# RWKV-7 scan in chunks of 64 tokens in place of 32, inside a two-layer hybrid diffusion block

## The chip, the cores and the metric

One NeuronCore of a Trainium2 chip runs the whole program: TensorE (PE) does the matrix products, VectorE (DVE), ScalarE (ACT) and GpSimd (POOL) the rest, SyncE (SP) and ACT issue the DMAs. The metric is the time of the whole program on the device in microseconds, smaller is better: 1599.16 us before, the median of three runs (1598.88 to 1600.44).

## The reference, cut to what matters

Two layers, each a mixer with four branches and a feed-forward part, are applied to 128 context tokens and 256 latent tokens. Branch A of the mixer is an RWKV-7 scan in both directions, with 4 heads of 64 channels. For each direction and head it is

```python
def step(S, inp):
    r_t, w_t, k_t, v_t, kk_t, a_t = inp
    s_a = jnp.einsum('dbhvk,dbhk->dbhv', S, -kk_t)
    S = (S * w_t[..., None, :] + s_a[..., :, None] * (kk_t * a_t)[..., None, :]
         + v_t[..., :, None] * k_t[..., None, :])
    return S, jnp.einsum('dbhvk,dbhk->dbhv', S, r_t)
S_fin, ys = lax.scan(step, S0, xs)
```

The context scan starts from zero, the latent scan from a cached state. The branches B, C and D are attentions; all four are multiplied by branch weights, gated, summed and projected.

## The kernel before, in words

All 384 tokens are worked on together. The large products (`gemm`, L686 to L688; the branch products, L882 to L884) split each fp32 weight tile into a high part (`whi`, made on ACT, L419) and a low part (`wlo_`, made on DVE or POOL, L421) and use three 128x128 products with 384 moving columns for each; below they are called **wide** products. `split_to` keeps four half tiles ready ahead of PE (HB = 4).

The mixer is a main generator (`main`: input projection, gates, branch products, in the order D, C, B, A) and two side generators, `side_rwkv` and `side_attention`. `run` advances the sides between steps of the main one; each `yield n` of a side says how many main steps it lets pass, stretched by PACE_RW or PACE_AT. The framework then orders the instructions of each engine; every engine runs its own list in order. Branch A is the last that `main` needs (`ready`, L870).

`side_rwkv` runs `rwkv_pair` for two pairs of heads in each layer, four times in all. In a pair, head 0 has its channels in partitions 0 to 63 and head 1 in 64 to 127 (`par` in the code). The tokens are cut into 12 chunks of 32 for each direction. The stages of a pair:

- **preparation** (L1230 to L1321): decays, their running sums, and the scaled keys. `KR` holds for each chunk 32 columns of kk and 32 of r (L1298, L1299), `BK` 32 columns of the b vectors and 32 of k (L1316, L1317).
- **chunk products** (L1327 to L1335): `AM` = BK^T KR for each chunk and head, 64x64, masked by L1334; then BK is transposed into `BKT` (L1344 to L1357), and `v` is loaded beside it into `UV`.
- **inverse** (L1336 to L1392): the 32x32 triangular block of each of 48 systems goes through DRAM into a layout with one system per partition, is inverted on DVE by 31 steps of a multiply (L1382) and a subtract (L1384), and goes through DRAM into `qt`.
- **scan** (L1399 to L1460): 8 steps. In steps 0 to 3 four scans are in flight (2 directions, latent and context), in steps 4 to 7 two. A step of n scans has five groups of 2n small fp32 products: KR^T S (L1409) and AM^T v (L1414) into one bank; copy to `rs` (L1417); qt^T rs (L1425); copy to UV with a minus (L1426 on ACT for head 0, L1427 on DVE for head 1); BKT^T UV (L1435) for the new state and AM^T u (L1442) for the outputs; then the state's sum and scaling (L1445, L1446) and the copy of the outputs (L1448).
- **end** (L1463 to L1511): both directions are added, normalised and gated; after branch C has been used, L1198 transposes the result for the branch product.

In the profile an fp32 product counts as two matmul instructions, so a group of 8 products is shown as x16.

Of the kernel before, what the change touches and what calls it, by code (L numbers as in the profile page):

```python
# [21 lines left out]
NP = 128  # L22
# [9 lines left out]
GATE_ORDER = (BR_D, BR_C, BR_B, BR_A)  # L32
LAG = 2
# [138 lines left out]
C_MASK, C_SCAN = 960, 1024  # L172
C_FLIP = 1408
NCONST = 1536


def constants():
# [29 lines left out]
    s = (p % 32)[:, None]  # L207
    j = np.arange(32)[None]
    c[:, C_MASK:C_MASK + 32] = s < j
    c[:, C_MASK + 32:C_MASK + 64] = s <= j  # L210
    c[:, C_SCAN:C_SCAN + NT] = (np.arange(NT) % 32 != 0)[None]
# [116 lines left out]
def build(tc, I, O):  # L328
# [451 lines left out]
    def mixer(l, x, xspill, hs, M, merged_of):  # L780
# [10 lines left out]
        vB = M.tile([128, 3, 384], F32, name="vB")  # L791
# [414 lines left out]
        def chunk(g, d, i):  # L1206
            if d == 0:
                return (4 + i) if g == 0 else i
            return i if g == 0 else 8 + i
# [7 lines left out]
        def slot0(i):  # L1217
            return i * 4 if i < 4 else 16 + (i - 4) * 2

        def rwkv_pair(pr):  # L1220
# [3 lines left out]
            def t6(name):  # L1224
                return M.tile([128, 2, 12, 64], F32, name=name, tag="t6", bufs=4)

            def flat(t, d):
                return t[:, d, :]
# [36 lines left out]
            gs = M.tile([128, 24], F32, name="gs", tag="gs", bufs=2)  # L1265
            for d in range(2):
                for g in range(2):
                    n = 8 if g == 0 else 4
                    if d == 0:
                        base, step = (128 + 31, 32) if g == 0 else (31, 32)  # L1270
                    else:
                        base, step = (352, -32) if g == 0 else (96, -32)
                    idx = g * 2 + d

                    def src(a, b):
                        lo = base + step * a
                        hi = base + step * (b - 1)
                        if step > 0:
                            return lw[:, d, 1 + lo:2 + hi:32]
                        return lw[:, d, 1 + hi:2 + lo:32][:, ::-1]  # L1280

                    V.tensor_copy(gs[:, idx:16:4], src(0, 4))
                    if g == 0:
                        V.tensor_copy(gs[:, 16 + idx:24:2], src(4, 8))
# [4 lines left out]
            def view(t, d, part):  # L1289
                v = t[:, d, :, part * 32:part * 32 + 32]  # L1290
                return v if d == 0 else v[:, ::-1, ::-1]

            def v3(a):
                return a.rearrange("p (c t) -> p c t", t=32)
# [18 lines left out]
            for d in range(2):  # L1313
                V.tensor_mul(a[:, d, :], a[:, d, :], kk)
                V.tensor_mul(kd[:, d, :], kd[:, d, :], kz)
                V.tensor_mul(view(bk_, d, 0), v3(a[:, d, :]), v3(ei[:, d, :]))  # L1316
                V.tensor_mul(view(bk_, d, 1), v3(kd[:, d, :]), v3(ei[:, d, :]))  # L1317
# [5 lines left out]
            am = t6("AM")  # L1323
            bt = t6("BKT")
            msk = cst[:, None, C_MASK:C_MASK + 64].to_broadcast([128, 8, 64])
            amf, btf = (t.rearrange("p d c j -> p (d c) j") for t in (am, bt))
            for bi in range(3):  # L1327
                ps = bk_rw().rearrange("p (c j) -> p c j", j=64)
                for s in range(8):
                    d, c = divmod(bi * 8 + s, 12)  # L1330
                    for par in range(2):
                        rows = slice(par * 64, par * 64 + 64)
                        T.matmul(ps[rows, s, :], bk_[rows, d, c, :], kr_[rows, d, c, :], start=True, stop=True)
                V.tensor_mul(amf[:, bi * 8:bi * 8 + 8, :], ps, msk)  # L1334
                yield 2  # L1335
            bd = PD.tile([48, 32, 32], F32, name="bd", tag="bd", bufs=2)  # L1336
            for par in range(2):
                dma(bd[par * 24:par * 24 + 24].rearrange("s r c -> r s c"), amf[par * 64:par * 64 + 32, :, 0:32])
            bm = e4([96, 32, 32], "bm")
            for h in range(2):  # L1340
                dma(bm[h * 48:h * 48 + 48], bd)
            q = e4([96, 16, 32], "q")
            dma(q.rearrange("p a b -> p (a b)"), I["eye"])
            for bi in range(3):  # L1344
                ps = bk_rw().rearrange("p (s q j) -> p s q j", q=2, j=64)
                for s in range(4):
                    d, c = divmod(bi * 8 + s * 2, 12)
                    T.transpose(ps[:, s].rearrange("p q j -> p (q j)"), bk_[:, d, c:c + 2, :], ident)
                out = btf[:, bi * 8:bi * 8 + 8, :].rearrange("p (s t) j -> p s t j", t=2)
                for par in range(2):  # L1350
                    for s in range(2):
                        o, i = out[par * 64:par * 64 + 64, :, s], ps[s * 64:s * 64 + 64, :, par]
                        if par:
                            V.tensor_copy(o, i)
                        else:
                            S.activation(o, i, AF.Copy)
                yield 3  # L1357
            uv = M.tile([128, 24, 64], F32, name="UV", tag="t6", bufs=4)
# [8 lines left out]
            for par in range(2):  # L1367
                rows = slice(par * 64 + 32, par * 64 + 64)
                for idx, (g, d) in enumerate(IDX):
                    base = first(g, d)  # L1370
                    src = vd[d][:, pr * 128 + par * 64:pr * 128 + par * 64 + 64]
                    dma(uv[rows, idx:16:4, :], src[base:base + 128].rearrange("(i s) v -> s i v", s=32))
                    if g == 0:
                        dma(uv[rows, 16 + idx:24:2, :],
                            src[base + 128:base + 256].rearrange("(i s) v -> s i v", s=32))
            yield 8

            tmp = M.tile([96, 272], F32, name="stmp", tag="stmp")
# [437 lines left out]
```

## Time and profile before

| | us |
|---|---|
| median of three runs | 1599.16 |
| the profiled execution, its own time | 1600.84 |
| its span, from first to last instruction | 1599.1 |
| PE busy | 1546.4 (97%) |
| PE weight loads busy | 1393.3 (87%) |
| DVE busy | 972.0 (61%) |
| ACT busy | 640.6 (40%) |
| POOL busy | 461.7 (29%) |
| granted TensorE clock, mean | 0.985 |

A busy PE is not PE at its peak: a matmul's duration holds the time until its end has left the array, and several overlap. What a group of small products costs PE is better read from when the next wide product starts.

### The profile page before, as it was taken

The page shows a single profiled execution, that of the slowest core. Times are in us where ns is not written, and L with a number is a line of the kernel's source. Part 1 is how long each engine was busy: PE and PEld are TensorE (multiplying, and loading weights), DVE is VectorE, ACT ScalarE, POOL GpSimd, SP SyncE. Part 2 cuts the span into 40 slices and gives each one's busy share as a digit, 9 for nine tenths or more (in the row PEclk, how much of TensorE's full clock was granted, in tenths as well). Part 3 has the DMA queues.
Part 4 walks back from the last instruction along what each step waited for, and adds up shares of the span by engine and source line. Part 5 has one row for each costly group of instructions (what it writes and reads, how often), then busy time and mean ns, then how long its engine had stood idle before and what let it go on. Part 6 is the DMA issues. An engine that isn't in the chain of part 4 may idle for free. (4 is left out here: it accounts for less than half of the span.)

```text
span 1599.1 us, 28341 instructions
## 1 busy us (share of the span) xinstructions
PE 1546.4 (97%) x10972; PEld 1393.3 (87%) x10972; DVE 972.0 (61%) x2165; ACT 640.6 (40%) x1364; POOL 461.7 (29%) x357
## 2 busy tenths in 40 slices
PE   8999999999998999999989999999999989999997
PEld 6988778777898999999988887786779989999997
DVE  6378458844458677763474774676554787844333
ACT  3454334432343544433345533433423435444331
POOL 2121002101236455644461100012012453433222
PEclk9999999999999999999989999999999989999999
DMA  9644343425542566653333542353344415533332
GB/s 334 202 123 131 96 137 107 137 90 160 164 148 73 188 203 207 216 158 119 113 124 116 156 128 84 101 144 109 95 139 144 155 60 209 184 132 125 121 127 76
DMA packets 106758, 225.30 MB, mean 141 GB/s; under 512 B 41280, under 2 KB 51584, under 8 KB 105728
## 3 DMA queue, kind: packets, MB, share of 16 engines
q1 hardware_dynamic: 76384, 124.99, 24.7%
q10 hardware_dynamic: 30240, 98.51, 19.2%
q8 instruction: 86, 1.41, 0.3%
q14 instruction: 48, 0.39, 0.1%
HBM read 214.38 MB, written 9.08 MB: 140 GB/s over the span
## 5 line engine op out<-in xcount | busy, mean ns | idle before, releaser
L419 ACT ACTIVATE whi<-raw 128x512 fp32r<-128x512 f32 (+2 forms) x580 | 346.0, 603 | 495.8 <-PE bank L687 269.4
L686 PE MATMUL bank<-hk,whi 128*128 128x384 f32 x1424 | 502.1, 353 | 2.1 <-DVE mg L1551 1.1
L687 PE MATMUL bank<-hk,whi 128*128 128x384 f32 x1424 | 482.2, 339 | 1.9 <-DVE hk L1521 1.9
L686 PEld LDWEIGHTS bank<-hk,whi 128*128 128x128 f32 x1424 | 268.8, 189 | 30.8 <-issue 20.2
L687 PEld LDWEIGHTS bank<-hk,whi 128*128 128x128 f32 x1424 | 269.1, 189 | 7.6 <-DVE hk L1521 3.2
L686 PE MATMUL bank<-hid,whi 128*128 128x384 f32 x352 | 119.2, 339 | 0.0
L687 PE MATMUL bank<-hid,whi 128*128 128x384 f32 x352 | 119.0, 338 | 0.0
L563 DVE SCALAR_TENSOR_TENSOR junk<-rawm,cb 128x1024 f32<-128x1024 f32 x64 | 93.4, 1460 | 0.5
L710 PE MATMUL bank<-hk,whi 128*128 128x384 f32 x192 | 63.6, 345 | 5.3 <-DVE hk L618 4.9
L708 PE MATMUL bank<-hk,whi 128*128 128x384 f32 x192 | 67.0, 349 | 1.4 <-ACT hk L610 1.2
L686 PEld LDWEIGHTS bank<-hid,whi 128*128 128x128 f32 x352 | 66.2, 188 | 0.0
L687 PEld LDWEIGHTS bank<-hid,whi 128*128 128x128 f32 x352 | 66.2, 188 | 0.0
L891 POOL TENSOR_TENSOR merged<-merged,gate 128x384 f32<-128x384 f32 x24 | 29.7, 1239 | 111.1 <-DVE gate L890 98.0
L1558 POOL TENSOR_TENSOR acc<-acc,sqo 128x384 f32<-128x384 f32 x42 | 51.5, 1237 | 31.7 <-ACT sqo L1548 15.7
L843 ACT ACTIVATE gate<-bank 128x384 f32<-128x384 f32 x64 | 31.1, 486 | 64.9 <-PE bank L688 57.4
L1762 DVE TENSOR_TENSOR hid<-th,hid 128x384 fp32r<-128x384 f32 x44 | 42.2, 959 | 22.5 <-ACT hid L1761 22.5
L1759 DVE SCALAR_TENSOR_TENSOR th<-th,bank 128x384 f32<-128x384 f32 x44 | 24.3, 552 | 39.4 <-PE bank L688 39.0
L911 ACT ACTIVATE prob<-bank,tiny 128x384 f32<-128x384 f32 (+1 forms) x56 | 27.2, 485 | 51.7 <-DVE tiny L910 45.3
L710 PEld LDWEIGHTS bank<-hk,whi 128*128 128x128 f32 x192 | 36.4, 191 | 7.7 <-DVE hk L618 5.9
L1551 DVE TENSOR_SCALAR mg<-bank,Q 128x128 f32<-128x128 f32 x64 | 23.6, 409 | 31.9 <-ACT sqo L1548 30.7
L708 PEld LDWEIGHTS bank<-hk,whi 128*128 128x128 f32 x192 | 37.6, 196 | 2.6 <-ACT hk L610 1.5
L890 DVE SCALAR_TENSOR_TENSOR gate<-gate,bank 128x384 f32<-128x384 f32 x48 | 26.4, 550 | 21.3 <-PE bank L884 21.0
(2019 smaller groups left out, 3583.4 us busy)
## 6 DMA issues: line engine op xcount, KB each, us to landing
raw<-in_w ACTq DMA_DIRECT2D x150, 512.0 KB, 3.7
raw<-in_w SPq DMA_DIRECT2D x108, 512.0 KB, 3.7
rawm<-in_wm SPq DMA_DIRECT2D x32, 512.0 KB, 3.4
raw<-in_w SPq DMA_DIRECT2D x41, 384.0 KB, 3.1
wm<-in_wm SPq DMA_DIRECT2D x16, 512.0 KB, 8.2
raw<-in_w ACTq DMA_DIRECT2D x32, 256.0 KB, 2.7
raw<-in_w ACTq DMA_DIRECT2D x15, 384.0 KB, 3.2
bt<-in_bt SPq DMA_DIRECT2D x8, 256.0 KB, 4.7
```

The source lines that it names most:

```text
L419: last_split[:] = [S.activation(hi[:, :w], raws[i][:, sl], AF.Copy)]
L563: V.scalar_tensor_tensor(junk, raw, 1.0, cb[:, g, :], op0=OP.mult, op1=OP.mult, accum_out=acc[:, t, g:g + 1])
L686: T.matmul(ps[:, :n], wh, xh, start=(k == 0), stop=False)
L687: T.matmul(ps[:, :n], wh, xl, start=False, stop=False)
L708: T.matmul(o, wh, xh, start=(i == 0), stop=False)
L710: T.matmul(o, wh, xl, start=False, stop=(i == 7))
L843: S.activation(gates[b, m], ps[:, :NT], AF.Tanh, scale=0.5)
L890: V.scalar_tensor_tensor(gt, gt, 1.0, ps[:, :NT], op0=OP.add, op1=OP.mult)
L891: (G if m % 2 else V).tensor_add(merged[:, m, :], merged[:, m, :], gt)
L911: S.activation(e[:, :n], src, AF.Exp, bias=nb, scale=scale, accum_out=sm)
L1558: (V if i == 1 else G).tensor_add(a, a, b)
L1762: last = V.tensor_sub(h[:, 1, :], th, h[:, 0, :].bitcast(F32))
```

## The change

The chunk length becomes CH = 64, with NC_ = 6 chunks for each direction.

- `KR` and `BK` hold 64 + 64 columns for each chunk. Which of the two halves holds kk and r (or b and k) differs between the heads: `put` writes each head by its own multiply over 64 partitions, so four multiplies become eight for each of KR and BK.
- `AM` is 128x128 for each chunk and head, by products of 64-row operands with 128 weight columns and 128 moving columns, head 0 into bank A and head 1 into bank B; six masking multiplies in place of three.
- The inverse on DVE is as before, of 48 blocks of 32x32, now two diagonal blocks for each 64x64 system. The block beside the diagonal is made by three rounds of 24 products of 32x32 (`small_products`).
- The scan has 4 steps, two with four scans and two with two. KR^T S and AM^T v have 64-row operands with 128 weight columns and go to a bank for each head; BKT^T UV has 128-row operands with 64 weight columns. `rs` is copied by ACT for head 0 and by DVE for head 1, the outputs by two copies on ACT.
- Buffers: AM has its own tag, the `t6` tag three buffers, the first weights of the modulation (`load_quarter`) are loaded into the tags `am`, `vB`, `t6` and `v4`. The DMAs of the inverse's blocks are 12 in place of 8, in smaller pieces; `yield 12` ahead of the scan becomes 4 + 2 + 2 + 2 + 8.

```diff
+CH, NC_ = 64, 6
+            def put(t, d, part, a, b):
+                for par in range(2):
+                    rows = slice(par * 64, par * 64 + 64)
+                    V.tensor_mul(view(t, d, part ^ par)[rows], v3(a)[rows], v3(b)[rows])
...
-                V.tensor_mul(view(kr_, d, 0), v3(kk), v3(cx[:, d, :]))
-                V.tensor_mul(view(kr_, d, 1), v3(rr), v3(lw[:, d, 1:385]))
+                put(kr_, d, 0, kk, cx[:, d, :])
+                put(kr_, d, 1, rr, lw[:, d, 1:385])
...
             for bi in range(3):
-                ps = bk_rw().rearrange("p (c j) -> p c j", j=64)
-                for s in range(8):
+                pss = [bk_rw("A"), bk_rw("B")]
+                for s in range(4):
                     for par in range(2):
-                        T.matmul(ps[rows, s, :], bk_[rows, d, c, :], kr_[rows, d, c, :], start=True, stop=True)
-                V.tensor_mul(amf[:, bi * 8:bi * 8 + 8, :], ps, msk)
+                        T.matmul(pss[par][:, s * 128:(s + 1) * 128], ordered(bk_, d, c, par), ordered(kr_, d, c, par),
+                                 start=True, stop=True)
+                for par in range(2):
+                    V.tensor_mul(am[:, par, bi * 4:bi * 4 + 4, :].rearrange("p c (q t) -> p c q t", q=2),
+                                 pss[par].rearrange("p (c q t) -> p c q t", c=4, q=2),
+                                 parts(msk, par)[:, None].to_broadcast([128, 4, 2, CH]))
...
+            def small_products(lhs, rhs, out, scale):
+                ps = bk_rw().rearrange("p (c j) -> p c j", j=32)
+                for c in range(12):
+                    for par in range(2):
+                        o = out(par, c)[1]
+                        T.matmul(ps[o, c, :], lhs(par, c), rhs(par, c), start=True, stop=True)
+                for par in range(2):
+                    dst, o = out(par, None)
+                    if par:
+                        V.tensor_scalar(dst, ps[o, 0:12, :], scale, None, op0=OP.mult)
+                    else:
+                        S.activation(dst, ps[o, 0:12, :], AF.Copy, scale=scale)
...
-            yield 12
-            for i in range(8):
-                n = 4 if i < 4 else 2
+            yield 8
+            for i in range(4):
+                n = 4 if i < 2 else 2
...
                 for idx, d, c, par in todo:
-                    T.matmul(ry[rows, idx, :], kr_[rows, d, c, :], sS[rows, idx, :], start=(idx == 0),
+                    T.matmul(ry[par][:, idx, :], ordered(kr_, d, c, par), sS[own(par), idx, :], start=(idx == 0),
                              stop=False, skip_group_check=True)
...
-                V.tensor_copy(rs[:, :n, :], ry[:, :n, :])
+                S.activation(rs[own(0), :n, :], ry[0][own(0), :n, :], AF.Copy)
+                V.tensor_copy(rs[own(1), :n, :], ry[1][own(1), :n, :])
...
+                for idx, d, c, par in todo:
+                    T.matmul(sp[own(par), idx, :], bt[:, par, d * NC_ + c, :], uv[:, par, s0 + idx, :], start=False,
+                             stop=True, skip_group_check=True)
```

## Rows read from the trace of the kernel before

**Rows 1.** Page: each engine's busy time, its share of the span and its instructions.
```profile
PE 1546.4 (97%) x10972; PEld 1393.3 (87%) x10972; DVE 972.0 (61%) x2165; ACT 640.6 (40%) x1364; POOL 461.7 (29%) x357
```
**Rows 2.** Stages: length; busy PE, PEld, DVE, ACT, POOL; granted clock, DMA share, GB/s.
```profile
155.00:225.00 70.00, 70.00 (x780) 52.84 (x779) 34.22 (x102) 25.45 (x68) 3.90 (x4) 1.00 0.35 104
225.00:320.00 95.00, 92.79 (x629) 74.70 (x630) 77.24 (x216) 42.92 (x97) 16.74 (x14) 1.00 0.45 129
1005.00:1107.00 102.00, 97.54 (x645) 76.24 (x644) 77.00 (x223) 42.41 (x100) 15.20 (x13) 0.97 0.42 118
```
**Rows 3.** Timeline of PE (start, length, line, tiles): first two groups, long scan step.
```profile
155.20 0.34 PE L688 MATMUL bank<-hk,wlo__1832 128*128 128x384 f32 x1
155.47 0.68 PE L1409 MATMUL bank<-S,KR 64*64 64x64 f32 x16
156.08 0.68 PE L1414 MATMUL bank<-UV,AM 32*64 32x64 f32 x16
...
156.97 0.34 PE L687 MATMUL bank<-hk,whi 128*128 128x384 f32 x1
```
**Rows 4.** Timeline of PE: the third group of a long step, between wide products.
```profile
188.58 0.33 PE L687 MATMUL bank<-hk,whi 128*128 128x384 f32 x1
188.75 0.34 PE L688 MATMUL bank<-hk,wlo__2090 128*128 128x384 f32 x1
189.02 0.64 PE L1425 MATMUL bank<-rs,qt 32*32 32x64 f32 x16
...
189.86 0.34 PE L687 MATMUL bank<-hk,whi 128*128 128x384 f32 x1
```
**Rows 5.** Timeline of PE: the last two groups of a long step.
```profile
347.41 0.33 PE L688 MATMUL bank<-hk,wlo__3961 128*128 128x384 f32 x1
347.67 0.68 PE L1435 MATMUL bank<-UV,BKT 64*64 64x64 f32 x16
...
349.13 0.33 PE L687 MATMUL bank<-hk,whi 128*128 128x384 f32 x1
```
**Rows 6.** Timeline of PE: the third group of a short step.
```profile
366.95 0.33 PE L884 MATMUL bank<-brY,wlo__4297 128*128 128x384 f32 x1
367.21 0.41 PE L1425 MATMUL bank<-rs,qt 32*32 32x64 f32 x8
...
367.83 0.34 PE L687 MATMUL bank<-hk,whi 128*128 128x384 f32 x1
```
**Rows 7.** Groups by shape on PE: the products of L1409 (busy, mean ns | idle).
```profile
L1409 PE MATMUL bank<-S,KR 64*64 64x64 f32 x384 | 18.7, 227 | 0.0
```
**Rows 8.** Timeline of PE: one product of L1442 ahead of its group.
```profile
355.50 0.29 PE L1442 MATMUL bank<-UV,AM 32*32 32x64 f32 x2
```
**Rows 9.** Timeline of PE: 64-row products with 128 weight columns, in attention.
```profile
159.39 0.34 PE L688 MATMUL bank<-hk,wlo__1905 128*128 128x384 f32 x1
159.66 0.49 PE L939 MATMUL bank<-z,z 64*128 64x128 f32 x4
...
160.36 0.34 PE L687 MATMUL bank<-hk,whi 128*128 128x384 f32 x1
```
**Rows 10.** Timeline of PE: 128 weight columns with two moving columns.
```profile
1177.49 0.72 PE L1472 MATMUL bank<-cst,z 128*128 128x2 f32 x6
1178.08 0.42 PE L686 MATMUL bank<-hk,whi 128*128 128x384 f32 x1
```
**Rows 11.** Groups by shape on DVE (busy, mean ns | idle before, releaser).
```profile
L1316 DVE TENSOR_TENSOR BK<-a,ei 128x384 f32<-128x384 f32 x8 | 5.5, 689 | 0.0
L1334 DVE TENSOR_TENSOR AM<-bank,cst 128x512 f32<-128x512 f32 x12 | 7.9, 681 | 1.2 <-PE bank L1333 1.1
L1417 DVE COPY rs<-bank 128x256 f32<-128x256 f32 x16 | 6.8, 422 | 14.6 <-PE bank L1414 14.6
```
**Rows 12.** Waits of PE: line, releaser, us in total, times, longest.
```profile
PE bank L1198 <- DVE z L1511: 3.4, 2, 2.2
```
**Rows 13.** Timeline of PE: first product of branch A in layer 0.
```profile
437.34 0.34 PE L882 MATMUL bank<-brY,whi 128*128 128x384 f32 x1
```

More of the change, by code (lines that the diff above doesn't have):

```diff
@@ L1416, in rwkv_pair @@
                 rs = M.tile([128, 4, 64], F32, name="rs", tag="rs")
-                V.tensor_copy(rs[:, :n, :], ry[:, :n, :])
+                S.activation(rs[own(0), :n, :], ry[0][own(0), :n, :], AF.Copy)
+                V.tensor_copy(rs[own(1), :n, :], ry[1][own(1), :n, :])
                 yield 2
-                up = bk_rw("B").rearrange("p (c j) -> p c j", j=64)
-                for idx in range(n):
-                    g, d = IDX[idx]
-                    c = chunk(g, d, i)
-                    for par in range(2):
-                        rows = slice(par * 64, par * 64 + 32)
-                        T.matmul(up[rows, idx, :], qt[rows, d * 12 + c, :], rs[rows, idx, :], start=True, stop=True)
@@ L1426, in rwkv_pair @@
-                S.activation(uv[0:32, s0:s0 + n, :], up[0:32, :n, :], AF.Copy, scale=-1.0)
-                V.tensor_scalar(uv[64:96, s0:s0 + n, :], up[64:96, :n, :], -1.0, None, op0=OP.mult)
-                yield 2
-                sp = bk_rw("B").rearrange("p (c j) -> p c j", j=64)
-                for idx in range(n):
-                    g, d = IDX[idx]
-                    c = chunk(g, d, i)
-                    for par in range(2):
-                        rows = slice(par * 64, par * 64 + 64)
-                        T.matmul(sp[rows, idx, :], bt[rows, d, c, :], uv[rows, s0 + idx, :], start=True, stop=True)
@@ L1436, in rwkv_pair @@
-                for idx in range(n):
-                    g, d = IDX[idx]
-                    c = chunk(g, d, i)
-                    for par in range(2):
-                        hi = slice(par * 64, par * 64 + 32)
-                        lo = slice(par * 64 + 32, par * 64 + 64)
-                        T.matmul(ry[lo, idx, :], am[hi, d, c, 32:64], uv[hi, s0 + idx, :], start=False, stop=True,
-                                 skip_group_check=True)
+                for idx, d, c, par in todo:
+                    T.matmul(up[other(par), idx, :], qt[own(par), d * NC_ + c, :], rs[own(par), idx, :], start=False,
+                             stop=True, skip_group_check=True)
@@ new lines, in rwkv_pair @@
+                S.activation(uv[other(0), 0, s0:s0 + n, :], up[other(0), :n, :], AF.Copy, scale=-1.0)
+                V.tensor_scalar(uv[other(1), 1, s0:s0 + n, :], up[other(1), :n, :], -1.0, None, op0=OP.mult)
+                yield 2
+                for idx, d, c, par in todo:
+                    T.matmul(sp[own(par), idx, :], bt[:, par, d * NC_ + c, :], uv[:, par, s0 + idx, :], start=False,
+                             stop=True, skip_group_check=True)
+                for idx, d, c, par in todo:
+                    T.matmul(ry[par][other(par), idx, :], am[other(par), par, d * NC_ + c, other(par)],
+                             uv[other(par), par, s0 + idx, :], start=False, stop=True, skip_group_check=True)
@@ L1602, in load_quarter @@
         def load_quarter(q):
-            for i in range(q * 4, q * 4 + 4):
-                t = M.tile([128, 2, 512], F32, name="wm", tag=("t6", "e4")[i % 2], bufs=4)
-                dma(t, I["wm0"][i].rearrange("p (k c) -> p k c", k=2))
+            three = M.tile([128, 3, 2, 512], F32, name="wm", tag="am") if q % 2 == 0 else None
+            for i in range(4):
+                if i == 3:
+                    t = M.tile([128, 2, 512], F32, name="wm", tag=("vB", "v4")[q % 2])
+                elif three is not None:
+                    t = three[:, i]
+                else:
+                    t = M.tile([128, 2, 512], F32, name="wm", tag="t6", bufs=3)
+                dma(t, I["wm0"][q * 4 + i].rearrange("p (k c) -> p k c", k=2))
                 wm.append(t)
```

167 lines of the change are left out of this document (93 added, 74 removed).

## The prediction

> **What bounds the kernel now.** I read the page's busy times first: PE is busy for 97% of the span, the next engine, DVE, for 61% [rows 1]. Then the busy times by stage. While the first pair of heads is scanned, PE is busy for all of 70.0 us and DVE for 34.2 [rows 2]; the other three scan stretches look alike. So a scan does not wait for its own chain of copies: the list on PE fills every wait with wide products, and an instruction taken from PE in that stretch shortens the program. In the stretches of preparation and inverse DVE is the busier one, 77.2 of 95 us and 77.0 of 102 in the two fullest, and PE has 2 to 4.5 us that are not busy [rows 2]. Last, I read the timeline of PE for what a group of small products costs, because its busy time does not say it. Wide products follow one another 0.17 to 0.18 us apart [rows 4]. A group's cost is therefore the time from the start of the last wide product before it to the start of the second one behind it, less two such steps (0.35). This takes in what is lost at the group's edges.
>
> **Scan, before.** The first two groups of a long step (four scans): 156.97 - 155.20 - 0.35 = 1.42 us [rows 3]. The third: 189.86 - 188.75 - 0.35 = 0.76 [rows 4]. The last two: 349.13 - 347.41 - 0.35 = 1.37 [rows 5]. The third group of a short step, with half the products, costs 367.83 - 366.95 - 0.35 = 0.53 [rows 6]. So eight instructions cost 0.23, that is 0.029 each, and the group itself 0.30. The two pairs of groups in a short step then cost 16 x 0.029 = 0.46 less, 0.96 and 0.91. A long step is 3.55 us, a short one 2.40. There are 16 of each (4 pairs x 4), which agrees with the 384 instructions of L1409 [rows 7]: 95.2 us.
>
> **Scan, after.** Eight steps of each kind. The third group, and the last two, have as many instructions as before and no more columns: 0.76 + 1.37, or 0.53 + 0.91. The first two groups are one now (both are 64 rows by 128 columns), with 32 or 16 instructions whose weights are twice as wide. The trace has no such product with 64 moving columns. From below: it costs as before, 0.029. From above: attention's four 64x128 instructions with 128 moving columns cost 160.36 - 159.39 - 0.35 = 0.62, less 0.30, or 0.08 each [rows 9]. Between them: on the whole array six instructions with two moving columns take 0.59 us from the first's start to the next wide product's, 0.098 each [rows 10], and with so few columns I read this as the load of 128 weight columns; two heads in two halves of the rows would halve it, 0.049. I take 0.055, close to that, since four instructions carry much of one start. The first groups then cost 0.30 + 32 x 0.055 = 2.06 and 0.30 + 16 x 0.055 = 1.18. A long step is 4.19, a short one 2.62, and 8 x 6.81 = 54.5 us. **The scan gives 40.7 us** (31 at 0.08, 51 at 0.029).
>
> Two things change that. A group that shares its gap with attention's products does not pay the whole 0.30, and 96 groups become 60 (a long or short step has five groups in three places, so 3 x 32 before, and 3 x 16 and 12 rounds after): I take back a third of 36 x 0.30, 4 us (0 to 7). And single products start ahead of their group, because one half of UV is ready before the other [rows 8]; there are 21 such, each 0.30 + 2 x 0.029 = 0.36, 7.6 us in all. Half the steps should halve them, but `rs` now also comes from two engines: I count 2 us of gain (from 7 of gain to 4 of loss).
>
> **Chunk products.** 32 instructions of 64 columns in each of 12 groups become 16 of 128 columns: 0.30 + 32 x 0.029 = 1.23 against 0.30 + 16 x 0.055 to 0.08 = 1.18 to 1.58. I count nothing (from 1 gained to 4 lost). The transposes are as many as before.
>
> **Rounds for the inverse.** 12 rounds of 48 instructions of 32x32 with 32 moving columns are new. The nearest row is L1425, 32x32 with 64 columns, 0.029 each, so 1.69 a round; half the columns could halve it, 1.00. I take the middle: **16 us lost** (12 to 20). The Trainium skill, "TensorE: Matmul & The Clock Gate", section "Wait — 56ns, not 53.3ns?", has a floor of some 25 ns from start to start however few the columns; by that 12 x (0.30 + 48 x 0.025) = 18 us, an estimate from the page, and the forecast would be 2 us later. No row here has so few columns in small tiles.
>
> **DVE.** Each pair has eight more multiplies, of 64 partitions but as many elements in each; at 0.689 [rows 11] 5.5 us. Three more masks at 0.681 are 2.0, three copies of the rounds at about 0.42 are 1.3 [rows 11]: 8.8 us in a stretch where DVE has about 18 of 95 free [rows 2]. The cover is this free time, and the four half tiles of weights that are split ahead. Each removed pair of scan steps takes DVE work away where there is enough of it. Since the new work stands in front of the chunk products and ahead of the splits in DVE's list, I count 1 us of PE waiting in each pair, 4 us (0 to 12). SP issues a few more small DMAs; only the side waits for them. Nothing in `main` waits for the side: in layer 0 the second scan is in its short steps at 367 us [rows 6], 70 us ahead of the first use of branch A [rows 13].
>
> **End of the side.** PE waits 3.4 us in two places for the last product of the second pair (L1198) [rows 12]. In each pair the side lets 60 main steps pass from the inverse to the scan's end (12 + 8 x 6) and will let 42 pass (18 + 4 x 6); it comes nearer to the point where it must wait for branch C anyway, with its data long there: 2 us of gain (0 to 3.4).
>
> **How the numbers follow.** -40.7 + 4 - 2 + 0 + 16 + 4 - 2 = -20.7 us. The profiled execution took 1600.84 us, so 1580.1; the median of the runs is 1.7 us lower, so I predict **1578.5**. This measurement can tell about 0.2%, 3.2 us, from no change. The forecast's own range, with not all bounds at one end, is 1567 to 1592; chance 0.58.
>
> **Rivals.**
> 1. *Loads of 128 rows are exposed* (0.13). L1435's new weights fill all rows, so a load cannot run beside the other head's product, as it can in half the rows now. Each of 8 x (16 + 8) instructions then pays a load of 64 columns, half of 0.098: 9.4 us, 1588. No row shows such weights with so few moving columns. The Trainium skill, "TensorE: Matmul & The Clock Gate", section "The mechanism", states this rule: a load overlaps running products only where the row group differs. No run here has shown it yet.
> 2. *Everything small is cheap* (0.10). Wide weights at 0.029, rounds at 1.00, no new waits on DVE: 10 + 4 + 4 + 1 us more, 1559. For it: rows 3, with 64 weight columns in both groups, and rows 5, with 64 and 32, cost nearly the same, so loads seem hidden today. Against it: rows 10.
> 3. *Wide loads come one after another* (0.06). If two heads' loads do not run side by side, each instruction of the first groups costs 0.098: 8 x 48 x 0.043 = 16.5, and the chunk products 12 x 16 x 0.043 = 8.3. That is 1603, slower. Against it: 0.08 in rows 9, with twice the moving columns.
> 4. *DVE becomes the bound in preparation and inverse* (0.13). There 77.2 + 8.8 would be 86 of 95 us, 91%. It decides when DVE falls behind by more than the split-ahead weights cover; the wide products then wait for `wlo_`. All of 4 x 8.8 us on the path in place of 4 is 31 more: 1609, slower. Half of it gives no change. For it: PE's lost time in these stretches; against it: DVE still has free time. I give 0.07 to half of it and 0.06 to all.
>
> That the change does not do what it says has no chance of its own: the instructions are counted in the code.
>
> The range that should hold 8 in 10 reaches to rival 1 and nearly to rival 2 and the light half of rival 4: 1562 to 1598. Faster by over 0.2%: 0.58 + 0.13 + 0.10 = 0.81. Within: 0.07. Slower: 0.06 + 0.06 = 0.12.
>
> **What would show it.** In the changed profile a long step's groups should cost about 2.1, 0.8 and 1.4 us; a first group at 1.2 or above 3 would mean rivals 2 or 3, a last one near 2 rival 1. A round should cost 1.0 to 1.7. The two heads' loads in the first group should start in pairs. In the stretch of preparation PE's waits for BK, AM or `wlo_` should add up to a few us; more than 15 would mean rival 4. The scan stretches should be about half as long, with PE still busy throughout. The forecast is wrong in its frame if PE is not full there.

## The result

The change is **slower: 1639.58 us** (median; 1635.94 to 1641.29) against 1599.02 for the kernel before, a ratio of 1.0252 (95% interval 1.0230 to 1.0273). The forecast was 1578.5 us, range 1562 to 1598. It was wrong in its sign, and 61 us from the time.

The page of the changed kernel, to be read beside [rows 1] (busy times, then forty slices of the span):

```profile
span 1638.7 us, 27226 instructions
...
PE 1566.1 (96%) x10396; PEld 1419.0 (87%) x10396; DVE 980.0 (60%) x2153; ACT 642.8 (39%) x1364; POOL 459.1 (28%) x357
...
PE   8999999899999999999989999999999989999997
...
PEclk9999997988999899999999999999999989999999
```

PE has 576 instructions fewer and is busy for 20 us longer. The reason stands in the last line: in three slices of layer 0's mixer (the 7th, 9th and 10th) the granted clock is below 0.9. The stages, to be read beside [rows 2] (same columns; the first scan, preparation and inverse of the second pair, the second scan, and two stretches inside):

```profile
180.00:216.00 36.00, 36.00 (x373) 26.99 (x372) 20.14 (x62) 16.47 (x48) 1.58 (x1) 1.00 0.26 71
216.00:338.00 122.00, 110.61 (x627) 88.20 (x623) 80.75 (x228) 43.84 (x98) 14.81 (x12) 0.90 0.37 106
338.00:391.00 53.00, 52.03 (x509) 40.08 (x508) 21.37 (x57) 17.68 (x48) 4.70 (x5) 0.84 0.23 69
260.20:284.00 23.80, 23.80 (x109) 20.21 (x109) 10.72 (x21) 2.79 (x6) 2.01 (x2) 0.50 0.09 20
352.40:362.50 10.10, 10.10 (x52) 8.39 (x53) 2.88 (x11) 1.84 (x7) 0.00 (x0) 0.50 0.16 52
```

The first scan is as short as forecast: 36 us in place of 70. But the preparation behind it takes 122 us in place of 95, and PE is not busy for 11 of them. Two stretches run at a granted clock of 0.50, that is 1.2 GHz in place of 2.4, with PE busy throughout.

To find where the time is, I booked all of PE's time between its first and its last product. Each product has the time from its start to the next product's start, less what PE waited. In a stretch at half clock, half of that is booked as lost. What a small group loses at its edges falls to "all other products". The two right columns are experiments that follow (us, one profiled execution each):

| | before | after | no rounds (e1) | heads in turn (e15) |
|---|---|---|---|---|
| scan products | 81.9 | 61.1 | 52.7 | 51.9 |
| chunk products | 13.0 | 17.4 | 18.3 | 18.0 |
| rounds | 0 | 12.7 | 0 | 12.3 |
| all other products | 1430.8 | 1426.2 | 1421.0 | 1426.8 |
| lost to half clock | 20.5 | 48.6 | 17.6 | 27.5 |
| waits of PE | 38.4 | 57.6 | 52.0 | 48.4 |

At full clock PE's work did fall, by 8 us. The waits (+19) and the half clock (+28) took that back more than five times over.

The prices of the single groups were read well. A round (timeline of PE: start, length, line, tiles, count):

```profile
340.59 0.34 PE L688 MATMUL bank<-hk,whi 128*128 128x384 f32 x1
340.86 0.94 PE L1421 MATMUL bank<-cst,qt 32*32 32x32 f32 x46
341.73 0.44 PE L689 MATMUL bank<-hk,wlo__3730 128*128 128x384 f32 x1
342.01 0.34 PE L687 MATMUL bank<-hk,whi 128*128 128x384 f32 x1
```

By the prediction's method that is 342.01 - 340.59 - 0.35 = 1.07 us (forecast 1.00 to 1.69). The first step of the second scan is another matter:

```profile
349.53 0.94 PE L1421 MATMUL bank<-qt,sq 32*32 32x32 f32 x46
350.40 1.10 PE L1467 MATMUL bank<-S,KR 64*128 64x64 f32 x8
351.34 1.05 PE L1470 MATMUL bank<-UV,AM 64*128 64x64 f32 x8
352.32 1.21 PE L940 MATMUL bank<-kh,qh 96*128 96x128 f32 x4
353.46 1.97 PE L1467 MATMUL bank<-S,KR 64*128 64x64 f32 x8
355.23 1.91 PE L1470 MATMUL bank<-UV,AM 64*128 64x64 f32 x8
357.07 1.07 PE L518 MATMUL bank<-raw,cs 128*32 128x256 f32 x6
358.07 0.69 PE L687 MATMUL bank<-hk,whi 128*128 128x384 f32 x1
```

In the source the two heads take turns, 32 instructions in two groups of 16. Here each group comes in two blocks of eight: first all of one head, on one half of the rows, then all of the other. Eight instructions take 351.34 - 350.40 = 0.94 us, 0.117 each, against the 0.055 of the forecast; behind 352.4 us, at half clock, 355.23 - 353.46 = 1.77, 0.22 each. From 347.48 to 358.07 no wide product runs. PE does not wait once between 344.38 and 358.07, and the clock falls all the same. Six of the 16 scan steps run in such blocks, among them the first step of three of the four scans (all but the first scan).

The other long stretch at half clock, 260 to 284 us, stands behind the largest wait (PE, then DVE and POOL in the same time):

```profile
256.30 0.34 PE L689 MATMUL bank<-hk,wlo__2953 128*128 128x384 f32 x1
260.11 2.66 PE L1344 MATMUL bank<-KR,BK 64*128 64x128 f32 x16 [3.48 <-DVE BK L1297]
```
```profile
257.38 1.11 DVE L1297 TENSOR_TENSOR BK<-a,ei 64x384 f32<-64x384 f32 x2
258.52 2.12 DVE L1297 TENSOR_TENSOR BK<-kd,ei 64x384 f32<-64x384 f32 x2
```
```profile
258.34 1.31 POOL L422 TENSOR_TENSOR wlo__3030<-raw,whi 128x512 fp32r<-128x512 f32 x1 [1.93 <-ACT whi L420]
```

The chunk products stand in PE's list ahead of wide products whose operands are there, and wait 3.48 us for the doubled multiplies into BK. Two of these take 1.11 us here, and the next two 2.12 beside an operation of POOL.

### The profile page after: what moved, and what is told of

The parts are those of the page before. It is cut to its first block, busy times and chain, and to the rows that moved or that the text cites. A ratio compares the mean times of both kernels' runs of the same rounds, so it can differ in the third digit from the quotient of the medians.

```text
span 1638.7 us, 27226 instructions
## 1 busy us (share of the span) xinstructions
PE 1566.1 (96%) x10396; PEld 1419.0 (87%) x10396; DVE 980.0 (60%) x2153; ACT 642.8 (39%) x1364; POOL 459.1 (28%) x357
## 4 chain that ended last, share of the span: by engine, by line
PE 71%; DVE 14%; DMA 5%; issue 4%; POOL 3%; ACT 2%; SPq 1%; ACTq 0%; DVEq 0%; POOLq 0%
PE bank L687 16%; PE bank L688 16%; PE bank L689 15%; DMA raw<-in_w 3%; PE bank L518 2%; PE bank L1467 1%; PE bank L711 1%; PE bank L709 1%; PE bank L710 1%; PE bank L940 1%; POOL acc L1602 1%; PE bank L1470 1%; PE bank L883 1%; DVE BK L1297 1%; PE bank L1344 1%
## 5 line engine op out<-in xcount | busy, mean ns | idle before, releaser
L687 PEld LDWEIGHTS bank<-hk,whi 128*128 128x128 f32 x1424 | 270.7, 190 | 27.2 <-issue 20.1
L688 PEld LDWEIGHTS bank<-hk,whi 128*128 128x128 f32 x1424 | 270.9, 190 | 7.1 <-DVE hk L1565 3.1
L711 PEld LDWEIGHTS bank<-hk,whi 128*128 128x128 f32 x192 | 35.8, 188 | 8.2 <-DVE hk L619 6.4
L967 ACT ACTIVATE pt<-bank 128x384 f32<-128x384 f32 (+1 forms) x72 | 29.3, 416 | 30.7 <-PE bank L965 27.1
L965 PE MATMUL bank<-cst,prob 128*128 128x128 f32 x168 | 31.3, 286 | 9.3 <-DVE prob L914 5.3
```

The lines of the kernel that those rows point to most:

```text
L687: T.matmul(ps[:, :n], wh, xh, start=(k == 0), stop=False)
L688: T.matmul(ps[:, :n], wh, xl, start=False, stop=False)
L711: T.matmul(o, wh, xl, start=False, stop=(i == 7))
L965: T.transpose(ps[:, j * 128:(j + 1) * 128], e[:, j * 128:(j + 1) * 128], ident)
```

## The experiments

Five theories were open. **A**: late operands make PE wait, and the clock falls behind the waits. **B**: the small products of the rounds bring the clock down. **C**: the heads that run one after the other cost. **D**: DVE's added work is the cause. **E**, formed after the first four runs: the rounds make each scan late, and a late scan is crowded in PE's list. Times are medians; "e" runs name the kernel.

**e1: the change without its rounds.**

```
-            small_products(...)   # three rounds
...
+            for par in range(2):
+                V.memset(qt[lo(par), :, 32:64], 0.0)
+            yield 6
```

> The changed kernel without its three rounds of 32x32 products: the upper right block of each 64x64 inverse is set to zero, so that part of the inverse is left out; the rest is as in the change. Theory A (the time went into waits of PE for late operands, and into the half clock that follows them): the rounds cost only their own slots, 12.7 us of PE time, so about 1627 us, and the half-clock stretch behind the wait for BK at 260 us stays. Rival B (the many small products of the rounds bring the clock down): of the 48.6 us that the half clock costs, the 28 that are new go too, so about 1599.

1580.49 us, 0.9892 of before (0.9863 to 0.9921). The rounds cost 59 us, although their slots on PE are 12.7. The page has full clock nearly everywhere, and the same first step takes turns:

```profile
PEclk9999999999998999999999999999999989999999
```
```profile
312.12 1.11 PE L1461 MATMUL bank<-S,KR 64*128 64x64 f32 x16
313.06 1.06 PE L1464 MATMUL bank<-UV,AM 64*128 64x64 f32 x16
314.05 1.56 PE L1158 MATMUL bank<-z,small 128*128 128x384 f32 x4
```

16 instructions take 313.06 - 312.12 = 0.94 us, 0.059 each. A is too small by far; B, C and E all remain, since without rounds no scan is late and none begins in blocks (of the 16 steps only two short ones, at 188.2 and 342.2 us, run in blocks).

**e2: the second head's first product leads.**

```
+                lead = first_of(*todo[1])
+                with tc.issue_after(lead.ins):   # all other products of L1467
...
```

> The changed kernel, with the first product of a scan step that of the second head, and all other first products of the step behind it in PE's list; so the two heads' products should alternate again. Rival C (the heads have a bank each; where the first head's bank is free earlier, its products run by themselves at 0.112 us each in place of about 0.055, and the stretches of 9 to 11 us without a wide product bring the clock down): some six steps lose 1.8 us each, and 33.7 us of half clock lie in or behind these stretches, worth 17 us: about 1613. Theory A: the waits stay and so does most of the time, 1632 to 1640.

1616.79 us, 23 less than the change, close to C's 1613. But the edit did only half of what it says: in the trace three long steps still run in blocks of eight, two of them the first of a scan (the texts on record count a mixed step with them). This pointed to e15.

**e3: six main steps more ahead of the chunk products.**

> The changed kernel with six more main steps between the last multiply of BK and the chunk products that read it. Theory A: the wait of 3.48 us for BK at 260 us goes, and with it the 24 us at half clock behind it (12 us lost), and some 3 us of smaller waits for BK and AM: about 1621. Rivals B and C: the clock falls elsewhere and only the waits go, 1632 to 1637.

1642.91 us, above both. The wait at 260 us is gone, and others take its place (4.32 us of a round for the last DMA of the inverse, 3.03 in attention). Removing this one wait gave nothing back.

**e4: the kernel before with its eight multiplies into KR and BK as two each.**

> The kernel before with each of its eight multiplies into KR and BK done as two of 64 partitions, the same results in the same place: the DVE work of the change without its products. Rival D (DVE's added work in the preparation is the cause, rival 4 of the prediction): PE waits for BK, AM and the split weights, 1610 to 1630. Theories A to C: PE loses no more than the 1 us in each pair that was predicted, 1598 to 1605.

1605.62 us against 1598.92, 1.0038 (1.0021 to 1.0055). These multiplies cost 6.7 us by themselves; the forecast had 4 for all of DVE's added work. D is no main cause.

**e5, e6, e7, e8.** e5 keeps the rounds, but nobody reads their result. e6 lets more main steps pass ahead of the rounds (16 in place of 4) and between a step's groups (4 in place of 2). e7 is e6 with e2. e8 has two products of 384 columns in each round:

```
-                for c in range(12):
-                        T.matmul(ps[o, c, :], lhs(par, c), rhs(par, c), ...)
...
+                    T.matmul(ps[o, 0:12, :], lhs(par, 0), rhs(par), ...)   # 384 columns
```

> The changed kernel with all 576 products of the rounds, but the third round writes its result to a tile that nobody reads, and the upper right blocks are set to zero ahead of the rounds; so that part of the inverse is left out and the scan does not wait for the rounds. Theory E (crowding: the rounds make the scan ready late, PE's list then puts scan steps and rounds together with hardly a wide product between them, and the clock falls in these stretches): the rounds cost their 12.7 us of PE time and nothing more, 1580.5 + 12.7 = 1593, with no stretch at half clock beside a scan. Rival B (the 32x32 products themselves bring the clock down): the half clock stays, 1620 to 1640.

> The changed kernel, complete, with 16 in place of 4 main steps ahead of the rounds and 4 in place of 2 between the groups of a scan step, so that the rounds and the first scan step no longer stand together in PE's list. Theory E: the 28 us of new half clock go, and some of the single-row scan products (up to 8): 1597 to 1612. Rival B: the rounds are all there and the clock falls as before, 1630 to 1640.

> The later scan of the run before, and the first product of each scan step that of the second head. Theory E with C: both gains, 1588 to 1600. Rival B: 1612 to 1617, as with the heads together alone.

> The changed kernel with two products of 32x32 weights and 384 moving columns in each round in place of 24 with 32 columns, and the third round's copies scaled by zero, so that the upper right blocks are zero (that part of the inverse is left out); the chain of waits and copies from the inverse to the scan is as long as in the change. Theory E: the rounds' own slots fall to some 4 us, but the scan is still late, so a crowded stretch at half clock stays in the second pair of layer 0 and costs 8 to 12 us: 1580.5 + 4 + 10 = about 1595. Rival B: no small products in the rounds, no half clock: 1581 to 1586.

e5 gave 1638.71 us, e6 1610.05, e7 1607.89, e8 1626.46. e6 lies in E's range, e7 and e8 in neither. e5 lies in B's range but does not decide for B, because its edit did not do what it was for: the scan waited for the rounds even though it did not use them. The two PSUM banks of this side are shared, and the rounds hold them (in e12 below, with the rounds in other banks, the scan does not wait). From the end of the inverse to the first scan product that reads it pass 10 to 13 us in the kernel before, 10 to 11 in e1, 26 to 31 in the change (read from the timelines). In all four scans of e5 and of e8 the first step runs in blocks (in e6 and e7 in two of the four); the clock is at half in it or just behind it in all four of e5 and in two of e8. So the half clock does not need the rounds' many small products (e8 has two in a round), and B in its plain form falls. e8's own rounds were dearer than I expected: with them the products outside the scan take 26.8 us more than in e1, and its time lies 46 us above e1's, not 15.

**e9, e10, e11.** e9 puts lateness into the kernel before: half of each scan's initial state, zero, makes three trips through DRAM, and one main step stands between groups in place of two. e10 and e11 give the rounds the banks of attention (`bk_at()` in place of `bk_rw()`), with more main steps around them, and the leading product of e2.

> The kernel before, complete, with the start of each scan held back (half of its initial state, which is zero, comes by three trips through DRAM behind the inverse) and one main step in place of two between the groups of a step. No product of PE is added. In PE's list a scan of 480 products now lies among 100 to 130 wide products, before among 140 to 180. Theory E (a scan that comes late is crowded in the list, and the crowded stretches lower the clock, whatever came before it): the half clock grows from 44 us to 90 or more and the time to 1620 to 1645. Rival B (only the rounds' small products do that) or a late scan without a price: 1599 to 1608.

> The change, complete, with the rounds in the banks that attention uses, so that the first two groups of a scan need not wait for them; 12 main steps ahead of the rounds in place of 4, 4 in place of 2 between the groups of a scan step, and the two heads' first products together. By PE's list no stretch is crowded any more. Theory E: the time of the change without rounds plus their slots, 1580.5 + 12.7 = 1593, and up to 10 more where the preparation of the second pair still waits for DVE: 1590 to 1603. If the half clock has another cause, 1607 to 1612, as with the later scan.

> As the run before, but 8 main steps ahead of the rounds and 4 ahead of the scan, so that the end of a pair stands where it stood in the kernel before (the last products of the pairs' output at 677, 1119, 3876 and 4320 wide products; before at 651, 1096, 3866 and 4297). By the list hardly a stretch is crowded. Theory E: 1588 to 1602, a few us below the run before if its late end costs anything. If the half clock has another cause: 1607 to 1615.

e9: 1614.56 us, 19 above the kernel before, but with 44.4 us at half clock as before (expected: 90 or more). In the old scan, whose heads share a bank, lateness and closer groups cost time without any more half clock. e10: 1615.66, above both of its ranges; e11: 1611.46, in the range for another cause. Their scans are not crowded and no step runs in blocks, yet both lie 1% above the kernel before. In e11 half clock in the mixers stands in or behind waits: 3.62 us for BK, 4.06 for AM's mask, 2.18 to 2.85 for the scan's output.

**e12, e13, e14.** e12 has the rounds' products without lateness: result unused, banks of attention. e13 has lateness without the products: no rounds, and two trips through DRAM ahead of half of the initial state. e14 is e11 with more main steps ahead of the second pair's chunk products and of the output's products.

> The changed kernel with the rounds in attention's banks, their result written where nobody reads it, and the upper right blocks set to zero (that part of the inverse is left out). All 576 products of the rounds are there, and the scan waits for none of them: in PE's list it stands where it stands without rounds (last output products at 596, 972, 3801 and 4176 wide products; without rounds at 594, 972, 3801 and 4176). Theory E (the rounds cost because they make the scan late): 1580.5 + 12.7 = 1593, and no more half clock beside the scans than without rounds. Rival B (their small products, close to the scan's, lower the clock wherever they stand): 1610 to 1640.

> The changed kernel without rounds (upper right blocks zero, that part of the inverse is left out); half of each scan's initial state, which is zero, comes by two trips through DRAM behind the inverse, so that the scan stands in PE's list as late as in the change or later (first products behind 553, 936, 3768 and 4156 wide products; in the change 538, 912, 3753 and 4110). No product of PE is added. Theory E: lateness alone brings a good part of the 59 us back: 1600 to 1620, with half clock beside scans. Rival B: 1581 to 1590.

> The run with the rounds in other banks, earlier, and two waits taken out: 6 main steps more ahead of the chunk products of the second pair in each layer, and 12 in place of 8 ahead of the products that read the scan's output. Complete. Theory A2 (the half clock that is left beside the mixers starts at waits of 2 to 4 us for BK and for the scan's output): of 37 us at half clock there 20 or more go, and 8 us of waits: 1594 to 1602. If it is not the waits: 1608 to 1615.

e12: 1597.37 us, 17 above e1 and close to E's 1593. e13: 1596.12, 16 above e1, between its two ranges and with no half clock beside a scan in its profile. The rounds without lateness cost little more than their slots, lateness without rounds 16; both together, in the change, cost 59. What is left, some 27 us, belongs to neither alone. In e12 and e13 no scan begins with a block of one head (later steps do: five in e12, two short ones in e13). e12's one profile is the slowest of its eleven executions, 1613.5 us, so only its order is read here. e14: 1608.83; the waits moved, they did not go.

**e15: the heads in turn.** The products of a step's first two groups are chained in the order of the source (the second group's follow in the same way):

```
+                prev = None
                 for idx, d, c, par in todo:
+                    with ExitStack() as order:
+                        if prev is not None:
+                            order.enter_context(tc.issue_after(prev.ins))
-                    T.matmul(ry[par][:, idx, :], ...)
+                        prev = T.matmul(ry[par][:, idx, :], ...)
...
```

> The changed kernel, complete, with the 16 first products of each scan step (8 in a short one) put behind one another in PE's list in the order of the source, so that the two heads take turns in every step; in the run with the heads together four first steps still ran head after head. Rounds, lateness and crowding are as in the change (first products of the scans behind 538, 907, 3757 and 4124 wide products; in the change 538, 912, 3753 and 4110). Theory C (what products and lateness together cost beyond the sum of the two, some 27 us, is the scan's products running head after head, on half of the rows, and the half clock there): 1580.5 + 17 + 16 = about 1613, with hardly any half clock at the first steps. If crowding does it with any products: 1625 to 1640.

**1599.66 us**, 1.0008 of before (0.9983 to 1.0032): 40 us less than the change, with the same instructions, and below both expectations. The rounds are there, and from the inverse to the first scan product that reads it still pass 24 to 32 us. The page's clock, PE's waits (us in total, times, longest; two of the change, the same two of e15) and the second long step of the second scan:

```profile
PEclk9999799999999999999989999999999999999999
```
```profile
PE bank L1530 <- DMA yb<-yd: 5.9, 3, 3.3
...
PE bank L1344 <- DVE BK L1297: 4.3, 2, 3.5
```
```profile
PE bank L1536 <- DMA yb<-yd: 2.9, 3, 1.3
...
PE bank L1344 <- DVE BK L1297: 1.7, 3, 0.9
```
```profile
347.47 0.33 PE L689 MATMUL bank<-hk,wlo__3828 128*128 128x384 f32 x1
347.73 1.11 PE L1471 MATMUL bank<-S,KR 64*128 64x64 f32 x16
348.67 1.06 PE L1475 MATMUL bank<-UV,AM 64*128 64x64 f32 x16
349.66 0.45 PE L687 MATMUL bank<-hk,whi 128*128 128x384 f32 x1
349.95 0.34 PE L688 MATMUL bank<-hk,whi 128*128 128x384 f32 x1
...
350.30 0.34 PE L687 MATMUL bank<-hk,whi 128*128 128x384 f32 x1
350.56 0.68 PE L1483 MATMUL bank<-rs,qt 64*64 64x64 f32 x16
...
351.46 0.34 PE L689 MATMUL bank<-hk,wlo__3828 128*128 128x384 f32 x1
```

The table above says where the 40 us were: 9 in the scan's products, 21 in the half clock, 9 in waits. Four of the change's stretches at half clock (from 352.4, 369.4, 994.1 and 1144.3 us, 34 us together, so 17 lost) begin in or just behind block steps, with no wait of PE shortly before; e15 has none of them. In the change the waits for BK and for the scan's output add up to 4.3 and 5.9 us, here to 1.7 and 2.9, though nothing was done about them. So some 26 us lie at the blocks themselves; whether and how the rest follows from them was not followed further.

The edit did more than end the blocks. In the change 10.6 and 9.0 us pass without a wide product at the first two steps of the second scan (from 347.5 and 363.4 us); in e15 there are at most 4.2 in that scan, because wide products stand between its groups again. Which of the two the clock answers to, the blocks or the missing wide products, no run separates. One long step of the first scan has 7.2 us without a wide product in both kernels, with the heads in turn, and its clock is 1.00 (the change, then e15; columns as in [rows 2]):

```profile
194.00:201.20 7.20, 7.20 (x106) 5.55 (x104) 2.55 (x8) 2.91 (x8) 0.23 (x1) 1.00 0.26 75
```
```profile
201.20:208.40 7.20, 7.20 (x105) 5.53 (x104) 2.37 (x8) 3.36 (x9) 0.01 (x1) 1.00 0.23 75
```

**e16, e17: less late.** e16 is e15 with 12 main steps in place of 4 ahead of the rounds; e17 also gives the rounds the banks of attention.

> The change, complete, with the heads in turn, and 12 in place of 4 main steps ahead of the rounds; the ends of the pairs stand at 618, 1032, 3825 and 4221 wide products (in the change 605, 975, 3813 and 4183). If lateness and crowding still cost the 16 us that lateness alone cost: 1585 to 1596, below the kernel before. If a later pair costs as much in its waits as the crowding did: 1597 to 1606.

> As the run before, and the rounds in the banks that attention uses, so that the first two groups of a scan need not wait for the rounds. If the wait for these banks is what lateness costs: 1583 to 1593. If not: as the run before, within 5 us.

e16: 1598.25 us, 1.0004 of before (0.9986 to 1.0021), in its second range and no better than e15. e17: 1618.52, 20 worse and outside both readings, for a cause that I did not follow; its four executions, 1607.4 to 1627.2 us, stand in the order of their mean clocks, 0.977 to 0.962. No complete version beat the kernel before: what the scan gives, the rounds and the longer preparation take.

## Why the prediction was wrong, point by point

**The frame held.** PE is full in the scans, as the rows of stages show, and the first scan is half as long (the second, with its rounds and half clock, is not: 53 us).

**Scan: right where the heads take turns.** A long step's groups cost 349.95 - 347.47 - 0.35 = 2.13 us, 351.46 - 350.30 - 0.35 = 0.81 and, elsewhere in e15 and e1, 1.42 (forecast 2.06, 0.76, 1.37); a short step's 1.24, 0.58 and 0.95 (1.18, 0.53, 0.91). From before to e1 the table's scan products and all other products fall by 29.2 + 9.8 = 39.0 us; the sum said 40.7 - 4 + 2 = 38.7. That the 9.8 are the groups' edges is my reading. The last two groups, in e1:

```profile
330.04 0.33 PE L689 MATMUL bank<-hk,wlo__3591 128*128 128x384 f32 x1
330.31 0.69 PE L1477 MATMUL bank<-UV,BKT 128*64 128x64 f32 x16
330.92 0.68 PE L1480 MATMUL bank<-UV,AM 64*64 64x64 f32 x16
...
331.81 0.34 PE L688 MATMUL bank<-hk,whi 128*128 128x384 f32 x1
```

**The step that failed** is one clause in the scan's price: "two heads in two halves of the rows would halve it", taken as given because the source alternates the heads. The list of PE does not follow the source. In turn, the two heads' weight loads start in pairs, as the prediction wanted (single instructions of e15: 347.730 and 347.737 us, then 347.838 and 347.845); in a block there is one load every 0.11 us (the change: 350.397, 350.506, 350.615). Each head now has a bank of its own; behind the rounds, which use the same two banks in turn, one of them comes free earlier, and the products of its head are put first, all together. That the banks are why is read from the code and from where it happens (first steps of scans behind rounds in these banks: three of four in the change, all in e5 and e8, none in e1, e10 to e13), and is not shown; for the blocks in later steps, three in the change and two in e1, no run names a cause. That the order costs is shown by e15: with the heads in turn 40 of the 61 us between forecast and result are gone.

**Rival 3 was the nearest.** It is this mechanism, loads that do not run side by side, with 0.098 each and 1603 us at a chance of 0.06. In a block it was 0.117. I had excluded it as a property of the chip, by [rows 9], and did not ask whether the order could bring it about. It also lacked the half clock, which cost more than the slots (21 against 9 us). A first group above 3 us, its sign, was there: 350.40 to 357.07, with one group of attention inside and its second half at half clock.

The Trainium skill, "TensorE: Matmul & The Clock Gate", section "LDWEIGHTS (loading the stationary operand)", gives a weight load as the number of columns over 1.2, in ns. For 128 columns that is some 107 ns, an estimate from the page; the 0.11 from load to load in a block agrees (the profile draws one such load 0.19 us long, beyond the start of the next). Section "The mechanism" of that page lets a load overlap running products only in another row group; 0.059 in turn and 0.117 in blocks agree, but the 128-row weights of a long step's last two groups, which leave no other row group, cost only 1.42 us in place of 1.37.

**Rounds: the price right, the place wrong.** By the prediction's method a round costs 1.07 us, and the pair of instructions that starts ahead of it 0.37 (at 338.2 us): about 12 x 1.44 = 17 us for 16 forecast. (The table books 12.7 as slots; the rest are edges, among the 5.8 us by which all other products grow from e1 to e15.) The 46 instructions of a round start 0.87 / 46 = 0.019 us apart. (The floor of some 25 ns from the Trainium skill, "TensorE: Matmul & The Clock Gate", section "Wait — 56ns, not 53.3ns?", does not hold for them.) But the prediction booked nothing for their place: "nothing in `main` waits for the side". They put 15 us or more between the inverse and the scan, in the scan's own banks. Once the heads take turns that costs little: e15 lies 1599.7 - 1580.5 = 19.2 us above e1, and 17 of that is the price itself. Lateness alone cost 16 us in e13 (later than the change by PE's list) and 19 in e9 (later by the timeline, and with closer groups); why e15 pays so much less is open. I never asked what a late side does to the list.

**DVE and the waits: under-sized.** From before to e1 the waits grow by 13.6 us where the sum had 4 - 2 = 2. The multiplies themselves were priced right (64 of them take 41.0 us in place of 20.5 for 32), but the chunk products that read BK stand right behind them in PE's list, so DVE's free time elsewhere in the stretch was no cover. The chunk products' waits for BK and AM grow from 1.1 to 6.7 us. The rest of the growth is not DVE's alone: 2.6 us for the last DMA of the inverse (its DMAs are 14 in the code, not 12), 2.3 more for the scan's output, while the 3.4 us at L1198 [rows 12] are gone, better than the 2 forecast; what remains lies in smaller waits and was not followed. Rival 4 names the place and over-prices it: its sign was more than 15 us of such waits, the change has 7.4, and e4 has 6.7 us for the multiplies.

**Chunk products:** forecast nothing, up to 4; measured 4.4 to 5.3. A group of 16 costs 1.30 us at best, with the heads in turn; most groups hold runs of one head, with 0.11 us from start to start, and cost 1.6 us or more. It is the same failure of the same clause, and e15, which chains the scan's products alone, leaves it.

**Rival 1 is refuted.** The weights of all 128 rows cost next to nothing extra: the last two groups of a long step take 331.81 - 330.04 - 0.35 = 1.42 us in place of 1.37 [rows 5], where the rival had 16 x 0.049 = 0.8 more. Rival 2 is too: the first group costs 2.13, not 1.23.

Together: without rounds the change gains 18.4 us where 36.7 were forecast (waits 11.6 short, chunk products 5.3, half clock 2.9 the other way, and 4 us between this profile and the median); the rounds cost 59.1 in place of 16; 40 of that go with the heads in turn, and the other 19 are near the forecast.

## What to carry to other kernels

A price for small products that share the array holds for an order, and a planner that sorts by readiness may give another: where two halves get banks of their own, look at the list for blocks of one half, and chain the products if you count on turns. Work that is inserted in a chain is paid for in its own slots and can be paid for once more in what stands behind it, above all if it borrows the buffers of the next step. Before sizing a change of small products, ask of each stretch without a wide product what the granted clock does there.

## What the runs showed of the hardware

- The same instruction (64 rows, 128 weight columns, 64 moving columns) took 0.059 us in turn on two row halves, 0.117 in blocks on one, and 0.22 in blocks at half clock.
- The granted clock went to half at 352.4 us, for 10 us, while PE had not waited since 344.38; no wide product had run since 347.48. In the stretch of e15 that answers to it (338.6 to 350.0), with the heads in turn and wide products in between, the clock was 1.00:

```profile
338.60:350.00 11.40, 11.38 (x143) 8.25 (x142) 5.63 (x20) 5.24 (x17) 0.00 (x0) 1.00 0.24 87
```

- One program's time goes with its mean clock, if loosely. Ten executions of e15 lie between 1593.1 us (mean clock 0.986) and 1610.9 (0.976), so its one profile at 0.980 is one case: it has 20 us at half clock from 173.4 us on, behind a wait of 0.98 us of a round for a copy. Whether the quicker executions have that too is not known.
- Two multiplies of 64x384 on DVE took 1.11 us alone and 2.12 beside an operation of POOL. In the change none of the 46 multiplies of L1297 without POOL beside them took over 0.56 us; of the 18 beside one, eight took 1.06 to 1.55 and ten did not suffer. Half the partitions saved nothing (0.55 us each, as for 128x384).
